# A hybrid decoder block on one core: a new order for the opening, and one output row stored in halves

## The chip, the cores and the metric

The kernel runs on one core of a Trainium2 chip. The metric is the device time of one execution in microseconds; the median of three runs of the kernel before is 907.87 us (907.3 to 908.28). The profile is of one further execution. Engines are named as the profile names them: PE is the matrix engine (TensorE), PEld its weight loads, DVE is VectorE, ACT is ScalarE, POOL is GpSimd, SP issues most transfers.

## The reference, cut to what matters

One residual block over 1024 tokens of width 1024, all in float32. The opening computes the modulation of the conditioning vector and the normalised, modulated input h; everything else starts from one large projection of h.

```python
def rmsnorm(x, g):
    r = lax.rsqrt(jnp.mean(xf * xf, axis=-1, keepdims=True) + NORM_EPS)
    return (xf * r).astype(x.dtype) * g

mod = c @ w_ada[l] + b_ada[l]
shift, scale, gate = jnp.split(mod, 3, axis=-1)
h = rmsnorm(x, norm_g[l]) * (1.0 + scale[:, None, :]) + shift[:, None, :]
proj = h @ w_in[l]
q, k, v, g_attn, xr, g_rnn, m_attn, m_rnn = jnp.split(proj, SPLIT_POINTS, axis=-1)
q = partial_rope(q, positions)           # ang = positions * inv_freq; cos, sin
k = partial_rope(k, positions)
# sliding-window attention with sinks, a conv and an RG-LRU, gates,
# two projections, one output projection
x = x + gate[:, None, :] * (merged @ w_out[l])
return rmsnorm(x, final_g)
```

## The kernel before, in words

**Numbers.** A float32 product is made of three products of rounded operands: each operand is split into a high part (hh for h, wh for weights) and a rest (hl, wl), and PE computes hh x wh, hh x wl and hl x wh. A product is of 128 x 128 weights with 512 columns. ACT (or POOL) makes the high part with a cast, DVE the rest with a subtraction. Weights come by half chunks of 128 x 512 in tiles named r.

**The opening** (lines 186 to 550) has its order written out by hand for all five engines: each engine executes its instructions in the order in which the code calls them, and waits where an operand is not there. Nothing overtakes.

- SP loads eight tiles of x (128 tokens each), a table of small parameters (pk_t), then in turns weight halves and the modulation matrix (wada, two tiles of 512 KB for each of eight blocks kc of 128 features). The positions (posr_t) come over POOL's queue.
- For each tile i of x: ACT squares and sums it (`square`, L365), DVE forms the mean plus epsilon (`mean`, L368), ACT takes the root (`root`, L372), DVE the reciprocal and scales the tile (`scaled`, L376 and L378), or, for the tiles in DIAG, scales an identity matrix (L382). PE transposes the tile in eight pieces into two sets of four PSUM banks (`flip`, L395, L397), and after two tiles ACT or DVE evicts the four banks (`out_of`, L403, L405) into xT.
- The conditioning vector is broadcast by PE (L264) and copied by DVE into c_bc. For each kc, DVE multiplies two wada tiles with it and sums (`modulate`, L275): one gives the shift, one the scale. The shift of kc 0 is made by PE instead (L451), in bank bk0. ACT turns them into a shift and a gain for each feature (`scales_of`, L280, L282).
- `hi_parts(kc)`: ACT writes the high part of h (L411, L413; in two halves of 512 tokens for kc below 4) and then h itself in place (L415). `lo_parts(kc)`: DVE writes the rest (L472, L475).
- `first(kc, terms, cs)`: PE multiplies feature block kc with the weights of four starting column chunks c = 0 to 3. Chunks 2 and 3 collect in the banks bk, chunks 0 and 1 in the banks pmain, which also serve the transposes. The first weight halves of the chunks serve kc 0 to 3, the second halves kc 4 to 7; the second ones are cast by ACT: chunk 0 ahead of kc 4's h, chunks 1 to 3 behind kc 5's h.
- KEEP_BUSY products with zeros (L454) stand on PE between the transposes and the first product.

**The angles.** POOL reduces the rope angles to one turn in 36 small operations (L305 to L356). The generator `angles()` is advanced by `turn(n)`: three at a time among the tiles, and the rest behind POOL's casts of two weight halves. ACT then takes the sine (L526), on its queue between h of kc 4 and the scales of kc 5. POOL stores the result and loads the tables that the rope needs.

**The end.** The eight output rows of 128 tokens are finished one after another; row 6 and row 7 overlap. ACT scales the right half of row 6 (L1965), DVE its left half (L1969), SP stores the row in one transfer. Row 7 is then scaled and stored in halves.

Of the kernel before, what the change touches and what calls it, by code (L numbers as in the profile page):

```python
# [22 lines left out]
P = 128  # L23
S = 1024
D = 1024
# [22 lines left out]
DIAG = 0, 2, 4  # L48
KEEP_BUSY = 4
# [5 lines left out]
def tile_hybrid_block(ctx, tc, x, pk, rows, posr, posi, c_row, w_ss, w_gate, w_main, w_v,  # L55
# [135 lines left out]
    with ExitStack() as st:  # L191
# [6 lines left out]
        dma(posr_t[:], posr, G)  # L198
# [34 lines left out]
        load_ss(0)  # L233
        for c in (0, 1):
            load_s(c, 0)
# [13 lines left out]
        warm = sp.tile([P, 1], F32, name="warm")  # L249
        V.memset(one_row[:], 1.0)  # L250
        zero = rbig[:, :HALF]
# [27 lines left out]
        def scales_of(kc):  # L279
            A.activation(shf[:, kc:kc + 1], mods[:, kc:kc + 1] if kc else bk[0][:, 0:1],  # L280
                         AF.Identity, bias=pcol(PK_BSH, kc))
            A.activation(gsc[:, kc:kc + 1], mods[:, 8 + kc:9 + kc], AF.Identity,  # L282
                         scale=pcol(PK_NG, kc), bias=bng[:, kc:kc + 1])

# [82 lines left out]
        def mean(i):  # L367
            V.tensor_scalar(out=rr[:, i:i + 1], in0=ss[:, i:i + 1], scalar1=1.0 / D, scalar2=EPS,  # L368
                            op0=ALU.mult, op1=ALU.add)

        def root(i):
            A.activation(rr[:, i:i + 1], rr[:, i:i + 1], AF.Sqrt)  # L372
# [16 lines left out]
        def flip(i):  # L389
            for kc in range(KC):  # L390
# [16 lines left out]
        def hi_parts(kc, between=lambda: None):  # L407
# [6 lines left out]
            between()  # L414
# [10 lines left out]
        late = {1: [lambda: V.tensor_copy(c_bc[:, SL[0]], psc[0]),  # L425
                    lambda: V.tensor_copy(c_bc[:, SL[1]], psc[1])],
                3: [lambda: out_of(0, 0, V), lambda: out_of(0, 1, V)],
                4: [lambda: out_of(0, 2, V), lambda: out_of(0, 3, A)],
                5: [lambda: out_of(1, 0, V), lambda: out_of(1, 1, V)],
                6: [lambda: out_of(1, 2, A), lambda: out_of(1, 3, A),  # L430
                    lambda: V.scalar_tensor_tensor(
                    out=bng[:], in0=pk_t[:, PK_BSC:PK_BSC + 8], scalar=1.0,
                    in1=pk_t[:, PK_NG:PK_NG + 8], op0=ALU.add, op1=ALU.mult)]}
# [12 lines left out]
        scaled(7)  # L446
        for p in range(4):
            out_of(2, p, A)
        flip(7)
        for k in range(KC):  # L450
            T.matmul(bk[0][:, 0:1], wada[0, 0][:, k * P:(k + 1) * P], pcol(PK_C, k),  # L451
                     start=(k == 0), stop=(k == KC - 1))
        for i in range(KEEP_BUSY):
            T.matmul(bk[1], zero[:, 0:P], zero, start=True, stop=True)  # L454
        for c in (2, 3):
            cast_s(c, 0, G)
        cast_s(0, 0)
        turn()
        modulate(0, (1,))
        for p in range(2):  # L460
            out_of(3, p, A)
        scales_of(0)
        hi_parts(0, lambda: cast_s(1, 0))
        for c in (2, 3, 0):
            rest_s(c, 0)
        modulate(1)
        csn = sp.tile([P, 3, 64], F32, name="csn")

        def lo_parts(kc):
            if kc < 4:  # L470
                for hf in range(2):
                    V.tensor_tensor(out=hl[kc][hf], in0=xT[kc][:, SL[hf]],  # L472
                                    in1=f32(hh[kc][hf]), op=ALU.subtract)
# [1583 lines left out]
```

## Time and profile before

| | |
|---|---|
| median of three runs | 907.87 us |
| the profiled execution | 907.33 us, its span 905.5 us |
| PE busy | 894.3 us, 99% |
| first product of the projection | 23.44 us |
| PE without a gap from | 28.07 us to the end of the opening |
| sine of the angles on ACT | 41.99 us |
| last product | 898.23 us |

Times in rows are microseconds from the span's start: start, duration, engine, line, operation, output and input by the program's names. A bracket tells how long the engine had been idle before, and what released it. In a table by stretches, each engine's busy time is followed by its number of instructions in brackets; the last three numbers are the granted PE clock, the share of the transfer engines and GB/s.

### The profile page before, as it was taken

The numbers are of one execution on the slowest core, as the hardware profiler recorded it, in microseconds if no ns is written. First come the engines' busy times: TensorE is split into PE (matmuls) and PEld (weight loads), VectorE is DVE, ScalarE is ACT, GpSimd is POOL, SyncE is SP. The second block draws the span as 40 slices with busy tenths as digits, with TensorE's granted clock in tenths as the row PEclk, the third lists the DMA queues.
The fourth block names the chain that finished last, engine by engine and source line by source line (L and its number), as shares of the span: only waits on it lengthen the run. The fifth ranks groups of instructions, "written<-read, shape, count | busy, mean of one in ns | idle before, by whom it ended". The sixth has DMA issues, their size and how long they took to land.

```text
span 905.5 us, 12663 instructions
## 1 busy us (share of the span) xinstructions
PE 894.3 (99%) x4259; PEld 746.1 (82%) x4259; DVE 718.6 (79%) x1073; ACT 567.2 (63%) x1098; POOL 121.1 (13%) x216
## 2 busy tenths in 40 slices
PE   8999999999999999999999999999999999999996
PEld 6789888888888888888888888888888888888885
DVE  6987688978669875987788597999999847569755
ACT  7965554654566855786585884888888732115435
POOL 6520241200000000000000002343433300000000
PEclk9999999999999999999999999999999999999999
DMA  9828489772435354354446367996656289316504
GB/s 356 338 69 285 165 256 321 256 234 95 151 128 182 121 208 135 124 183 163 158 140 214 105 203 248 349 404 208 215 199 207 74 310 363 140 47 234 207 1 186
DMA packets 87205, 180.74 MB, mean 200 GB/s; under 512 B 8626, under 2 KB 29122, under 8 KB 87140
## 3 DMA queue, kind: packets, MB, share of 16 engines
q1 hardware_dynamic: 83056, 167.07, 52.3%
q0 software_dynamic: 3936, 12.59, 4.3%
q8 instruction: 34, 0.56, 0.3%
q14 instruction: 31, 0.25, 0.1%
q10 hardware_dynamic: 148, 0.27, 0.1%
HBM read 121.34 MB, written 58.95 MB: 199 GB/s over the span
## 4 chain that ended last, share of the span: by engine, by line
PE 93%; DVE 4%; ACT 2%; issue 1%; DVEq 0%; ACTq 0%
PE bk L709 48%; PE rp L173 13%; PE out L1861 6%; PE pmain L173 5%; PE pgate L1025 5%; PE s_ps L1330 3%; PE pv L1403 3%; PE pmain L485 2%; PE bk L485 2%; PE pt L1369 1%; PE pmain L1580 1%; PE pmain L1579 1%; PE pmain L1578 1%; ACT jk L1879 1%; DVE xo L1875 1%
## 5 line engine op out<-in xcount | busy, mean ns | idle before, releaser
L709 PE MATMUL bk<-nh,wh 128*128 128x512 f32 x368 | 143.3, 389 | 0.0
L709 PE MATMUL bk<-nl,wh 128*128 128x512 f32 x368 | 143.2, 389 | 0.0
L709 PE MATMUL bk<-nh,wl 128*128 128x512 f32 x368 | 98.4, 389 | 0.0
L111 DVE TENSOR_TENSOR wl<-r,wh 128x512 fp32r<-128x512 f32 x109 | 75.0, 695 | 24.0 <-ACT wh L105 23.7
L105 ACT CAST wh<-r 128x512 fp32r<-128x512 f32 x107 | 65.5, 618 | 31.0 <-PE rp L173 11.1
L709 PEld LDWEIGHTS bk<-nh,wl 128*128 128x128 f32 x368 | 69.1, 188 | 14.4
L709 PEld LDWEIGHTS bk<-nl,wh 128*128 128x128 f32 x368 | 69.1, 188 | 14.2
L709 PEld LDWEIGHTS bk<-nh,wh 128*128 128x128 f32 x368 | 69.1, 188 | 14.2
L709 PE MATMUL bk<-hl,wh 128*128 128x512 f32 x184 | 71.6, 389 | 0.0
L709 PE MATMUL bk<-hh,wh 128*128 128x512 f32 x184 | 71.6, 389 | 0.0
L111 DVE TENSOR_TENSOR wl<-ws,wh 128x512 fp32r<-128x512 f32 x76 | 52.1, 687 | 7.1 <-ACT wh L105 7.0
L62 POOL DMA_DIRECT2D yh_d<-av x1 | 0.6, 567 | 371.3 <-ACT av L1092 371.3
L1355 ACT ACTIVATE p<-p,small 128x129 f32<-128x129 f32 x128 | 50.0, 396 | 0.0
L709 PE MATMUL bk<-hh,wl 128*128 128x512 f32 x184 | 49.2, 389 | 0.0
L105 ACT CAST wh<-ws 128x512 fp32r<-128x512 f32 x76 | 46.0, 614 | 4.3 <-PE bk L709 2.1
L709 PEld LDWEIGHTS bk<-hh,wl 128*128 128x128 f32 x184 | 34.5, 188 | 7.2
L709 PEld LDWEIGHTS bk<-hl,wh 128*128 128x128 f32 x184 | 34.6, 188 | 7.1
L709 PEld LDWEIGHTS bk<-hh,wh 128*128 128x128 f32 x184 | 34.5, 188 | 7.1
L1330 PEld LDWEIGHTS s_ps<-ks,qs 128*128 128x128 f32 x256 | 34.4, 189 | 3.7 <-DVE p L1345 1.1
L1330 PE MATMUL s_ps<-ks,qs 128*128 128x256 f32 (+1 forms) x256 | 35.3, 280 | 0.6 <-DVE p L1345 0.6
L709 PE MATMUL bk<-hha,wh 128*128 128x512 f32 x92 | 35.8, 389 | 0.0
L709 PE MATMUL bk<-hla,wh 128*128 128x512 f32 x92 | 35.8, 389 | 0.0
(378 smaller groups left out, 2289.3 us busy)
## 6 DMA issues: line engine op xcount, KB each, us to landing
r<-w_main SPq DMA_DIRECT2D x100, 256.0 KB, 4.2
wada<-w_ss SPq DMA_DIRECT2D x16, 512.0 KB, 9.0
qs<-q_d SPq DMA_DIRECT2D x16, 512.0 KB, 4.9
wo_d<-wr SPq DMA_DIRECT2D x28, 256.0 KB, 3.0
wo<-wo_d SPq DMA_DIRECT2D x14, 512.0 KB, 5.1
ks<-k_d SPq DMA_DIRECT2D x12, 384.0 KB, 4.3
xt<-x SPq DMA_DIRECT2D x8, 512.0 KB, 7.0
sma_d<-c SPq DMA_DIRECT2D x16, 256.0 KB, 4.4
```

What stands on the lines that cost most here:

```text
L105: A.copy(dst[0][:], src)
L111: V.tensor_tensor(out=dst[1][:], in0=src, in1=f32(dst[0][:]), op=ALU.subtract)
L173: mm = T.matmul(ps[hf], ww, xx[kc][hf], start=(kc == 0 and ww is w_h and xx is xh), stop=(kc == KC - 1 and xx is xl))
L485: T.matmul(starts[c][hf], ww[:, c0:c0 + P], xh[kc][hf], start=(kc == 0 and t_ == "h"), stop=(kc == KC - 1 and t_ == "l"))
L709: W["pe"] = T.matmul(ps, ww[:, kc * P:(kc + 1) * P], b[kc][i], start=(first and n == 0), stop=(n == 11), skip_group_check=not first)
L1025: W["pe"] = T.matmul(ps[:, SL[hf]], ww[:, c0:c0 + P], xx_[:, SL[hf]], start=(ic == 0 and i == 0), stop=(ic == 1 and i == 2))
L1330: W["pe"] = T.matmul(o, qs[:, j, qc], ks[:, kb:n % 2 + 2, b, :], start=(b == 0), stop=(b == 1))
L1355: A.activation(px[:, j, :], px[:, j, :], AF.Exp, bias=sm[:, 0, j:j + 1], accum_out=sm[:, 1, j:j + 1])
L1369: W["pe"] = T.transpose(pt[:, j, :], px[:, j, 0:P], ident[:])
L1403: W["pe"] = T.matmul(pv[:], b, m[:].rearrange("p j q -> p (j q)"), start=(i == 0), stop=(i == len(prods) - 1))
L1578: T.matmul(o, hh[kc][th][:, ts_], wh[:, cols], start=(kc == 0), stop=False)
L1861: T.matmul(o, a[k][x_][:, p * P:(p + 1) * P], b[k][y_][:, cols], start=(first and k == 0 and i == 0), stop=(k == 3 and i == 2), skip_group ...
```

## The change

- `mean` is gone: `root` computes the square root of sum / D + eps itself, with eps in a small tile, and follows its square directly on ACT.
- The order among the tiles of x: roots in groups, evictions in other places, two diagonal tiles in place of three, two filler products in place of four. `flip` writes a bank's two halves in sequence.
- The shift of kc 0 is computed by PE ahead of tiles 6 and 7, in a bank of pmain, and finished by ACT behind the evictions.
- The first h (kc 0) is made, and multiplied, by halves of 512 tokens; POOL casts the first weight halves of all four chunks, and computes bng.
- The positions are loaded over SP's queue; all angles stand behind POOL's four casts.
- Row 6 is stored in two halves, the right one first.

The places at which instructions move, engine by engine. POOL, from its setup to the first angles (posf, ang, t, a, sa, sb, sc are the angles' tiles; wh are high parts of weights). Before:

```order
L62 DMA posr_t<-posr 128x65
masks.py:197 MEMSET ident 128x128
masks.py:199 ISA
masks.py:199 AFFINE_SELECT ident<-ident 128x128
L305 CAST posf<-posr_t 128x64
L307 TENSOR_SCALAR ang<-posf,posr_t 128x64
L291 TENSOR_SCALAR t_324<-ang 128x64
```

and further on, in the middle of the angles:

```order
L297 TENSOR_TENSOR a_411<-a_356,t_409 128x64
L322 TENSOR_SCALAR tmp<-t_409 128x64
L224 CAST wh<-r 128x512 x2
L326 TENSOR_TENSOR sa<-sa,tmp 128x64
L322 TENSOR_SCALAR tmp<-t_409 128x64
```

With the change:

```order
masks.py:199 AFFINE_SELECT ident<-ident 128x128
L469 TENSOR_SCALAR bng<-pk_t 128x8
L471 TENSOR_TENSOR bng<-bng,pk_t 128x8
L223 CAST wh<-r 128x512 x4
L313 CAST posf<-posr_t 128x64
L315 TENSOR_SCALAR ang<-posf,posr_t 128x64
L299 TENSOR_SCALAR t_463<-ang 128x64
L305 TENSOR_TENSOR a_465<-ang,t_463 128x64
```

The load is gone from this queue, and the 18 operations that stood ahead of the two casts stand behind four.

ACT, from the last root to kc 1's scales (hha and hhb are the high parts of h by token halves). Before:

```order
L372 ACTIVATE rr<-rr 128x1 x2
L403 COPY xT<-bk_68 128x2x256
L403 COPY xT<-bk_69 128x2x256
L403 COPY xT<-bk_70 128x2x256
L403 COPY xT_194<-bk_71 128x2x256
L105 CAST wh<-r 128x512
L403 COPY xT<-pmain 128x2x256 x2
L280 ACTIVATE shf<-bk_68,pk_t 128x1
L282 ACTIVATE gsc<-mods,bng,pk_t 128x1
L411 ACTIVATE hha_161<-xT,shf,gsc 128x512
L411 ACTIVATE hhb_162<-xT,shf,gsc 128x512
```

With the change:

```order
L376 ACTIVATE rr<-ss,eps 128x1
L407 COPY xT_194<-pmain 128x2x256
L407 COPY xT<-pmain 128x2x256
L407 COPY xT<-bk_70 128x2x256
L407 COPY xT<-bk_68 128x2x256
L407 COPY xT_194<-bk_71 128x2x256
L407 COPY xT<-bk_69 128x2x256
L282 ACTIVATE shf<-pmain,pk_t 128x1
L286 ACTIVATE gsc<-mods,bng,pk_t 128x1
L481 ACTIVATE hha_161<-xT,shf,gsc 128x512
L407 COPY xT<-pmain 128x2x256
```

Six evictions now stand between the last root and the first shift, the last two tiles' evictions and the second half of h behind it.

PE, from the shift's products to the first products with h. Before:

```order
L395 MATMUL pmain<-ident,xt 128x128 x16
L451 MATMUL bk_68<-pk_t,wada 128x1 x8
L454 LDWEIGHTS rbig
L454 MATMUL bk_69<-rbig 128x512
```

With the change, and with the buffers' numbers (pmain_198 holds the shift and half of each transposed tile):

```order
L461 MATMUL pmain_198<-pk_t_75,wada_232 128x1 x8
L399 MATMUL pmain_197<-ident_76,xt_223 128x128 x4
L399 MATMUL pmain_198<-ident_76,xt_223 128x128 x4
L399 MATMUL pmain_197<-ident_76,xt_225 128x128 x4
L399 MATMUL pmain_198<-ident_76,xt_225 128x128 x4
L468 LDWEIGHTS rbig_78
L468 MATMUL bk1_69<-rbig_78 128x512
```

The shift's products have moved ahead of tiles 6 and 7, whose pieces share a bank with it. PE's order from the second product with kc 1's rest on, ACT's and DVE's from kc 2's scales on, are as they were, but for a few casts and additions near the end of the kernel that the scheduler has placed otherwise.

The diff, cut to its core:

```diff
-DIAG = 0, 2, 4
-KEEP_BUSY = 4
+DIAG = 0, 2
+KEEP_BUSY = 2
...
-        dma(posr_t[:], posr, G)
...
         load_ss(0)
+        dma(posr_t[:], posr)
         for c in (0, 1):
             load_s(c, 0)
...
+        V.memset(eps[:], EPS)
...
-        def mean(i):
-            V.tensor_scalar(out=rr[:, i:i + 1], in0=ss[:, i:i + 1], scalar1=1.0 / D, scalar2=EPS,
-                            op0=ALU.mult, op1=ALU.add)
-
         def root(i):
-            A.activation(rr[:, i:i + 1], rr[:, i:i + 1], AF.Sqrt)
+            A.activation(rr[:, i:i + 1], ss[:, i:i + 1], AF.Sqrt, scale=1.0 / D, bias=eps[:])
...
-            for kc in range(KC):
+            for kc in (0, 4, 1, 5, 2, 6, 3, 7):
...
-        turn(3)
...
-        for i in range(8):
-            square(i)
-            mean(i)
-            if i:
-                root(i - 1)
-                scaled(i - 1)
-                if i < 6:
-                    turn(3)
-                flip(i - 1)
-            for f in late.get(i, ()):
-                f()
-        root(7)
+        norm(0, 1)
+        scaled(0)
+        scaled(1)
...
+        norm(7)
+        evict(1, v=(0, 1), a=(3, 2))
         scaled(7)
-        for p in range(4):
-            out_of(2, p, A)
+        m00 = starts[1][1][:, 0:1]
+        for k in range(KC):
+            T.matmul(m00, wada[0, 0][:, k * P:(k + 1) * P], pcol(PK_C, k),
+                     start=(k == 0), stop=(k == KC - 1))
+        evict(2, a=(2, 0, 3, 1))
+        shift_of(0, m00)
+        flip(6)
         flip(7)
...
-        for c in (2, 3):
+        for c in (2, 3, 0, 1):
             cast_s(c, 0, G)
-        cast_s(0, 0)
         turn()
         modulate(0, (1,))
...
+        hi_half(0, 0)
+        first(0, "hw", (2, 3), (0,))
+        evict(3, a=(0,), v=(2,))
+        affine_half(0, 0)
+        modulate(1, (0,))
+        rest_s(0, 0)
+        rest_s(1, 0)
+        modulate(1, (1,))
+        first(0, "hw", (0, 1), (0,))
+        hi_half(0, 1)
...
     A.activation(xo[6][:, RIGHT], xo[6][:, RIGHT], AF.Copy, scale=r6)
+    dma(out[6 * P:7 * P, RIGHT], xo[6][:, RIGHT])
...
-    dma(out[6 * P:7 * P, :], xo[6][:])
+    dma(out[6 * P:7 * P, LEFT], xo[6][:, LEFT])
```

More of the change, by code (lines that the diff above doesn't have):

```diff
@@ L449, in tile_hybrid_block @@
+        for k in range(KC):
[4 more added lines that the diff above has]
+        flip(6)
         flip(7)
-        for k in range(KC):
-            T.matmul(bk[0][:, 0:1], wada[0, 0][:, k * P:(k + 1) * P], pcol(PK_C, k),
-                     start=(k == 0), stop=(k == KC - 1))
         for i in range(KEEP_BUSY):
             T.matmul(bk[1], zero[:, 0:P], zero, start=True, stop=True)
-        for c in (2, 3):
+        G.tensor_scalar(out=bng[:], in0=pk_t[:, PK_BSC:PK_BSC + 8], scalar1=1.0, scalar2=None,
+                        op0=ALU.add)
@@ L476, in lo_parts, with first @@
                                 op=ALU.subtract)
-        def first(kc, terms, cs=range(N_ST)):
+        def first(kc, terms, cs=range(N_ST), halves=range(2)):
             for c in cs:
@@ L483, in first @@
                     ww, xh = {"h": (h, hh), "w": (l, hh), "l": (h, hl)}[t_]
[L484 removed]
+                    for hf in halves:
                         T.matmul(starts[c][hf], ww[:, c0:c0 + P], xh[kc][hf],
```

94 lines of the change are left out of this document (57 added, 37 removed).

## The prediction

> **What bounds the kernel now.** I read the page's busy shares first, then TensorE's (PE) timeline of the opening, then the engines that end its waits.
>
> ```profile
> span 905.5 us, 12663 instructions
> PE 894.3 (99%) x4259; PEld 746.1 (82%) x4259; DVE 718.6 (79%) x1073; ACT 567.2 (63%) x1098; POOL 121.1 (13%) x216
> PE 93%; DVE 4%; ACT 2%; issue 1%; DVEq 0%; ACTq 0%
> ```
>
> PE is busy 99% of the span and holds 93% of the chain that ended last. So an edit counts only if it moves PE's first matmuls, opens a gap in PE, or moves what follows PE at the end. PE's matmul order behind the first three contraction chunks (kc 0 to 2) does not change.
>
> ```profile
> 23.44 0.47 PE L485 MATMUL bk<-hha,wh 128*128 128x512 f32 x1 [0.68 <-ACT hha L411]
> ...
> 28.07 0.39 PE L485 MATMUL bk<-hha,wh 128*128 128x512 f32 x1
> 28.30 0.40 PE L485 MATMUL bk<-hhb,wh 128*128 128x512 f32 x1
> ...
> 48.04 0.62 PE L485 MATMUL pmain<-hh,wh 128*128 128x512 f32 x2
> ```
>
> The input projection starts at 23.44. The row at 28.07 is its 15th matmul; from there on one starts every 0.227 us (28.07 to 28.30, and 88 steps from 28.07 to 48.04). With no gap at all the stream would have begun at 28.07 - 14 x 0.227 = 24.9: I call that the effective start. The row at 48.04 is matmul 102 (counted from 0): the first of kc 4 for column chunk 1, and the first that needs that chunk's second weight half.
>
> **The opening itself.** Its chain is squares and roots on ScalarE (ACT), scaling on VectorE (DVE), transposes on PE, evictions, first h.
>
> ```profile
> 7.98 1.06 ACT L365 ACTIVATE junk<-xt 128x1024 bf16<-128x1024 f32 x1 [0.93 <-DMA xt<-x]
> 8.95 0.18 ACT L365 ACTIVATION_READ_ACCUMULATOR junk<-xt 128x1 f32 x1
> ...
> 17.29 0.20 ACT L372 ACTIVATE rr<-rr 128x1 f32<-128x1 f32 x1 [0.47 <-DVE rr L368]
> 17.86 2.06 ACT L403 COPY xT<-bk 128x512 f32<-128x512 f32 x4 [0.36 <-PE bk L395]
> ...
> 884.84 0.29 ACT L1890 ACTIVATE rbig<-rbig 128x1 f32<-128x1 f32 x1
> ```
>
> The mean goes into the root, and each root stands right behind its square. The last row is such a root at the kernel's end: 0.29 us. A square with its accumulator read takes 1.15 (7.98 to 9.13), so a tile takes about 1.42. Six tiles from 7.98 and one eviction (2.06 / 4 = 0.51) end at 17.0, against 17.49 (17.29 + 0.20). Six evictions follow (3.1), then the first shift (0.2): 20.3.
>
> ```profile
> 18.23 1.97 PE L395 MATMUL pmain<-ident,xt 128*128 128x128 f32 x16
> 21.74 1.02 PE L454 MATMUL bk<-rbig 128*128 128x512 bf16 x4
> ```
>
> The shift's eight small products now stand ahead of the last two tiles' transposes, in a bank these need, so half of tile 6's transposes wait for the shift: 20.3. Left are one and a half tiles (1.97 / 2 each, 1.5) and two filler matmuls (half of 1.02): 22.3 for the first matmul, 1.1 earlier. Its h half is ready at about 21.5 and waits.
>
> ```profile
> 14.44 1.28 DVE L405 COPY xT<-pmain 128x512 f32<-128x512 f32 x2
> ...
> 18.27 0.75 DVE L378 TENSOR_SCALAR xt<-xt,rr 128x1024 f32<-128x1024 f32 x1
> 18.94 1.26 DVE L275 SCALAR_TENSOR_TENSOR jk<-wada,c_bc 128x1024 bf16<-128x1024 f32 x1
> 20.13 2.16 DVE L111 TENSOR_TENSOR wl<-r,wh 128x512 fp32r<-128x512 f32 x3
> ```
>
> DVE decides next. It scales tile 7 until about 18.8 (19.02 before), does the first modulation (1.26) and two low weight halves (0.7 each) to 21.4, evicts a bank when tile 7 is transposed (21.8 to 22.5, 0.64 as in the first row), then one modulation and two low halves: 25.1. Matmul 7 needs the last: effective start 25.1 - 7 x 0.227 = 23.5. **The opening alone is worth 1.4 us**, if nothing stalls later. Bounds: 2.6 (24.9 - 22.3, DVE not limiting) and 0 (DVE held 0.6 by each of the two casts that go to GpSimd, POOL). The rest costs nothing on PE: the transposes' new order, fewer diagonal multiplications (DIAG) and the sum bng on POOL lie ahead of the 22.3 beside ACT's chain.
>
> ```profile
> 4.70 0.94 SPq L62 DMA_DIRECT2D pk_t<-pk  x1
> 11.75 0.33 SPq L62 DMA_DIRECT2D r<-w_main  x1
> ...
> r<-w_main SPq DMA_DIRECT2D x1, 256.0 KB, 7.3
> ```
>
> The positions' load moves from POOL's queue into SP's, ahead of the first halves of chunks 0 and 1. A like load (first row) issues in 0.94. Chunk 0's half, issued at 11.75, lands at 19.05; up to 0.94 later is still ahead of the 20.1 at which DVE ends its modulation. Covered; without that cover it is the 0.94.
>
> **Where it is lost: the angles.** Of the 36 POOL operations that make the rope angles, 18 stood ahead of two weight casts and 18 behind; now all stand behind four casts.
>
> ```profile
> 6.32 0.46 POOL L307 TENSOR_SCALAR ang<-posf,posr_t 128x64 f32<-128x64 f32 x1
> ...
> 14.20 0.40 POOL L322 TENSOR_SCALAR tmp<-t 128x64 f32<-128x64 f32 x1
> 15.17 1.28 POOL L224 CAST wh<-r 128x512 fp32r<-128x512 f32 x2 [0.57 <-DMA r<-w_main]
> ...
> 20.45 0.78 POOL L291 TENSOR_SCALAR ra<-sa 128x64 f32<-128x64 f32 x1
> ...
> 31.97 1.03 POOL L356 TENSOR_SCALAR trn<-trn 128x128 f32<-128x128 f32 x1
> ```
>
> ```profile
> 5.90:14.70 8.80, 8.33 (x56) 6.36 (x56) 7.06 (x21) 7.75 (x20) 7.41 (x18) 1.00 1.02 401
> 20.40:33.00 12.60, 11.42 (x54) 8.37 (x54) 12.21 (x19) 11.95 (x22) 11.56 (x13) 1.00 1.03 402
> 109.90:120.40 10.50, 10.50 (x48) 8.71 (x47) 10.40 (x18) 7.65 (x14) 9.12 (x17) 1.00 0.69 230
> ```
>
> The windows' counts (third bracket DVE, fifth POOL) are the argument. From 5.9 to 14.7, while DVE copies from PSUM, scales and idles, POOL does 18 operations in 8.63 us: 0.48 each. From 20.4 to 33.0 DVE runs operations with two SBUF inputs (19, five of them accumulator reads), and POOL does 13 in 12.6 us: 0.97 each, one per DVE operation. From 109.9 to 120.4 it is 17 beside 18, on tiny 128x8 operands: lockstep again, so size is not the cause. In the changed kernel all 36 fall into this second regime.
>
> ```profile
> 41.99 0.31 ACT L526 ACTIVATE csn<-trn 128x128 f32<-128x128 f32 x1
> ...
> 45.52 1.65 ACT L105 CAST wh<-r 128x512 fp32r<-128x512 f32 x3
> ```
>
> ```profile
> 44.03 1.22 DVE L275 SCALAR_TENSOR_TENSOR jk<-wada,c_bc 128x1024 bf16<-128x1024 f32 x1
> ...
> 46.16 1.90 DVE L111 TENSOR_TENSOR wl<-r,wh 128x512 fp32r<-128x512 f32 x3 [0.90 <-ACT wh L105]
> ```
>
> The fourth cast (0.61 each, behind DVE's modulation) ends near 21.4. DVE then has 24 two-input operations and one eviction up to its modulation of kc 6, which ended at 45.2 and ends at about 46.5 now (0.5 for its later kc 2, 0.8 for POOL beside 11 more: the three at 20.13 took 2.16 with POOL, the three at 46.16 took 1.90 without). After that DVE needs casts that ACT does behind the sine, so it idles and POOL runs at 0.48. POOL: 26 done by 46.5, 10 x 0.48 more: **51.5**. The sine has waited until then; it ran at 41.99 with its input ready at 33.0 (31.97 + 1.03). Queued behind it on ACT are kc 5's scales, its h, and the three casts. So chunk 1's cast moves with it: 4.14 behind the sine (45.52 + 0.61 - 41.99), now 55.6. PE wanted it at 48.04, 1.9 after its end at 46.13. **Delay of PE against before: 51.5 - 41.99 - 1.9 = 7.6**; the opening's 1.4 only makes PE stand 9.0 instead. Bounds: 0.48 throughout gives 38.7, no stall; 0.97 to the end gives 56.3.
>
> ```profile
> 62.95 0.68 DVE L617 TENSOR_TENSOR c<-pmain,ctab 128x512 f32<-128x512 f32 x1
> ```
>
> Behind the angles in POOL's queue stand the transfers of the rope tables. They move by the sine's 9.5, and their first use, the row above, which waited for nothing, moves with PE by 9.3: no second stall.
>
> **The clock.** A gap of 9 us has its own price.
>
> ```profile
> 1.38 4.55 PE L256 MATMUL bk<-rbig 128*128 128x512 bf16 x12 [1.38 <-DVE warm L258]
> ...
> 898.23 0.28 PE L1861 MATMUL out<-wo,ml 128*128 128x256 f32 x1
> ```
>
> ```profile
> 903.00:904.00 1.00, 0.00 (x0) 0.00 (x0) 0.00 (x0) 0.00 (x0) 0.00 (x0) 0.50 0.75 273
> 900.00:901.00 1.00, 0.00 (x0) 0.00 (x0) 0.94 (x3) 0.72 (x1) 0.00 (x0) 1.00 0.00 0
> 901.00:902.00 1.00, 0.00 (x0) 0.00 (x0) 0.00 (x0) 0.00 (x0) 0.00 (x0) 1.00 0.98 393
> ```
>
> PE's last matmul is that of 898.23; the granted clock (third number from the end) is 1.00 to 902 and 0.50 from 903. At the start, 12 products of 512 columns take 4.55, a pitch of 0.38 where 0.227 is full speed: about 8 of them at twice the pitch, some 1.7 us lost until the clock is up. PE idle for 9 us falls to half and pays that again: **1.7**, bounds 0 and 2.0.
>
> **The end.** Row 6 is stored in two halves. Its right half is ready early, in a stretch where the DMA engines are idle (DMA share 0.00 from 900 to 901).
>
> ```profile
> 898.70 0.72 ACT L1965 ACTIVATE xo<-xo,rbig 128x512 f32<-128x512 f32 x1 [0.23 <-DVE rbig L1964]
> ```
>
> It can go at 899.4. Then 256 KB fewer stand before row 7's, 0.67 us at 393 GB/s; but row 7's own halves go no earlier, as their scaling is not touched. Bounds 0 and 0.67; I take **0.3**, halfway.
>
> **Sum.** On the profiled execution (907.33 us, span 905.5): +7.6 +1.7 -0.3 = +9.0, 916.3. The median of the runs shown is 907.87, 0.54 higher, inside their spread.
>
> The Trainium skill, "SBUF — State Buffer", section "SBUF: two separate sides", says that VectorE and GpSimd share a port pair as an exclusive lock: an operation with two SBUF inputs, or a GpSimd operation, holds it for its whole length and the other blocks fully. The trace agrees for POOL (13 beside 14). For DVE it does not: three operations take 0.26 longer beside POOL, 0.09 each, not POOL's 0.48.
>
> **Rivals.**
> - Faster: the angles are ready in time, because POOL slips more than one operation between two of DVE. The sine must not start later than 41.99 + 1.9 - 1.4 = 42.5, which leaves 21.1 us for 36, 0.59 each. Then 907.33 - 1.4 - 0.3 = 905.6. For it: the 0.48 of the early window, and a POOL that is busy 13% of the span. Against: both lockstep windows, at 0.97 and 0.62 with the smallest operands. Chance 0.09.
> - Slower by less: 0.70 per operation, midway. Sine at 46.6, PE 4.6 - 1.9 = 2.7 late after a gap of 4.1, at the edge of the clock's fall (half of 1.7): 910.6. Chance 0.10.
> - Slower by more: POOL stays at 0.97 after DVE has gone idle. Sine at 56.3, 14.3 - 1.9 + 1.7 - 0.3: 921. Against: the early window. Chance 0.06.
> - DVE waits out each POOL operation: 24 x (0.48 - 0.09) = 9.4 later, 925.7. That is the skill's lock to the letter, and the rows above are against it. Chance 0.02.
> - No change: something ahead of the sine that I price at nothing is itself late, or the angles miss by the 1.7 that the opening gains. Chance 0.03.
> - The forecast: 0.70.
>
> **Numbers.** Faster or slower counts from 0.2%, 1.8 us, which a measurement can tell from no change. Faster 0.09, same 0.03, slower 0.88. The forecast's own range is 913.5 to 918.5: sine 1.5 either way, the clock's 0 to 2.0. To hold 8 in 10 the range takes in the second rival and stops short of the third: 909.5 to 920.
>
> **What would show it.** POOL's angles begin near 21.4 and end near 51.5, at 0.9 to 1.0 each until 46; ACT idles about 9 us ahead of the sine, released by POOL; DVE idles ahead of its low halves; PE has one gap of about 9 us ahead of kc 4's second chunk, near 46.7 to 55.7, with a granted clock below 1 in it and behind; the first matmul is near 22.3. A sine near 41 and no gap would refute the whole; a gap without a fall of the clock, only the 1.7.

## The result, and the profile after

The changed kernel takes 917.33 us (median of five runs, 916.64 to 918.17); the kernel before takes 907.9 in the same set (907.3 to 908.93). The ratio is 1.0104, with a 95% interval from 1.0089 to 1.0119: 1% slower. The forecast was 916.3, in a range of 909.5 to 920. The profiled execution took 917.33 too, with a span of 915.5 against 905.5.

The page of the changed kernel, with its span, busy times and the chain that ended last:

```profile
span 915.5 us, 12637 instructions
PE 896.7 (98%) x4248; PEld 748.0 (82%) x4249; DVE 718.5 (78%) x1066; ACT 568.2 (62%) x1096; POOL 131.5 (14%) x219
PE 89%; POOL 3%; DVE 3%; DMA 2%; ACT 2%; issue 1%; SPq 0%; DVEq 0%; ACTq 0%
```

PE is busy for about as long as before. What is new is 3% of POOL in the chain, which runs through the angles, until now on no path that counted, from 20.8 to 51.3. PE's timeline in the changed kernel shows where PE stood because of it:

```profile
46.59 0.62 PE L509 MATMUL pmain<-hh,wh 128*128 128x512 f32 x2
...
47.50 0.61 PE L509 MATMUL pmain<-hl,wh 128*128 128x512 f32 x2
55.51 1.22 PE L509 MATMUL pmain<-hh,wh 128*128 128x512 f32 x2 [7.39 <-ACT wh L105]
56.52 1.05 PE L509 MATMUL pmain<-hh,wl 128*128 128x512 f32 x2
...
61.96 0.63 PE L509 MATMUL pmain<-hh,wh 128*128 128x512 f32 x2
```

Followed backwards: the row at 55.51 waits 7.39 us for a cast of ACT, the cast stands on ACT behind the sine, and the sine waits for POOL. The rows of ACT, DVE and POOL in the changed kernel:

```profile
51.34 0.31 ACT L556 ACTIVATE csn<-trn 128x128 f32<-128x128 f32 x1 [8.13 <-POOL trn L364]
...
54.85 1.64 ACT L105 CAST wh<-r 128x512 fp32r<-128x512 f32 x3
```

```profile
55.48 1.90 DVE L111 TENSOR_TENSOR wl<-r,wh 128x512 fp32r<-128x512 f32 x3 [8.30 <-ACT wh L105]
```

```profile
20.81 0.69 POOL L313 CAST posf<-posr_t 128x64 f32<-128x64 int32 x1
...
46.16 1.26 POOL L347 TENSOR_SCALAR tmp<-a 128x64 f32<-128x64 f32 x1
47.50 0.32 POOL L350 TENSOR_TENSOR sc__461<-sc__461,tmp 128x64 f32<-128x64 f32 x1
...
50.77 0.53 POOL L364 TENSOR_SCALAR trn<-trn 128x128 f32<-128x128 f32 x1
```

POOL's first angle starts at 20.81, behind two casts that wait for a weight half to land (18.97), and its last ends at 51.30. Up to 47.42 it did 29 of the 36 (0.92 each); from 47.50, with DVE idle since 47.18, the last seven took 0.54 each. From 23.44 on, when DVE is past its wait for the transposes, it is 24 operations of POOL beside 24 of DVE with two inputs in SBUF. A TENSOR_TENSOR of 128x64 takes 0.32 alone and 0.5 to 1.2 beside DVE.

For the account, PE's rows of the kernel before that answer to these, and a landmark at which the projection's first stage is over:

```profile
46.68 0.62 PE L485 MATMUL pmain<-hh,wh 128*128 128x512 f32 x2
...
52.12 0.62 PE L485 MATMUL pmain<-hh,wh 128*128 128x512 f32 x2
...
68.44 0.28 PE L1578 MATMUL pmain<-wh,hha 128*128 128x256 f32 x1
```

| landmark on PE | before | after | later by |
|---|---|---|---|
| first product of kc 4 (chunk 0) | 46.68 | 46.59 | -0.09 |
| first product with chunk 1's second half | 48.04 | 55.51 | 7.47 |
| first product of kc 5 | 52.12 | 61.96 | 9.84 |
| first product of the next stage (pmain<-wh,hha) | 68.44 | 78.29 | 9.85 |
| last product | 898.23 | 908.82 | 10.59 |
| end of the span | 905.5 | 915.5 | 10.0 |

So the opening, with all its new order, is worth 0.09; the wait for the angles costs 7.56; the 18 products behind it, at the lower clock, cost 2.37; 0.74 is lost between the end of the first stage and the last product; and the end is 0.59 shorter. Each profile is one execution: the sixth experiment below has the opening of the kernel before, unchanged, and its profile reaches kc 4 at 46.11, 0.57 earlier. So a few tenths in the opening cannot be told from one pair of profiles; 7.56 and 2.37 can.

### The profile page after: what moved, and what is told of

The parts are those of the page before. It is cut to its first block, busy times and chain, and to the rows that moved or that the text cites. A ratio compares the mean times of both kernels' runs of the same rounds, so it can differ in the third digit from the quotient of the medians.

```text
span 915.5 us, 12637 instructions
## 1 busy us (share of the span) xinstructions
PE 896.7 (98%) x4248; PEld 748.0 (82%) x4249; DVE 718.5 (78%) x1066; ACT 568.2 (62%) x1096; POOL 131.5 (14%) x219
## 4 chain that ended last, share of the span: by engine, by line
PE 89%; POOL 3%; DVE 3%; DMA 2%; ACT 2%; issue 1%; SPq 0%; DVEq 0%; ACTq 0%
PE bk L739 48%; PE rp L173 13%; PE out L1891 6%; PE pmain L173 5%; PE pgate L1055 5%; PE s_ps L1360 3%; PE pv L1433 3%; PE pt L1399 1%; PE bk L509 1%; PE pmain L509 1%; DMA xt<-x 1%; PE pmain L1610 1%; PE pmain L1609 1%; PE pmain L1608 1%; DMA r<-w_main 1%
```

## The experiments

Each is compared with runs of the kernel before on the same chip: medians 907.32 (experiments 1, 2, 4 and 5), 907.47 (3, 6, 7 and 8), 907.72 (9 and 10) and 907.69 (11 and 12).

**1. The angles back to an early place.** The changed kernel, with the positions loaded over POOL's queue at the start and 18 angle operations ahead of bng and the four casts.

```diff
         posr_t = sp.tile([P, 65], I32, name="posr_t")
+        dma(posr_t[:], posr, G)
...
         load_ss(0)
-        dma(posr_t[:], posr)
...
+        turn(18)
         G.tensor_scalar(out=bng[:], in0=pk_t[:, PK_BSC:PK_BSC + 8], scalar1=1.0, scalar2=None,
```

> The changed kernel with one part undone: the positions are loaded over POOL's queue at the start again, and 18 of the 36 angle operations stand ahead of POOL's sums and casts. Theory (the angles behind the casts run in lockstep with DVE and hold the sine): the angles end near 38, the sine does not wait, PE has no gap ahead of kc 4's second chunk. The opening's effective start was 24.83 with the change and 24.9 before, so it gives 0.1, the row in halves 0 to 0.3: 907.0, between 906 and 908. Rival (the order by token halves or the clock's fall in the opening is what costs): the angles matter little and it stays above 914.

Measured: 908.99 (908.5 to 910.49), ratio 1.0018 (1.0009 to 1.0027). It is 1.67 above the kernel before of its own set, where the changed kernel was 9.4 above: 7.8 of the 9.4 us are gone. The last angle and the sine in this kernel:

```profile
35.47 0.53 POOL L364 TENSOR_SCALAR trn<-trn 128x128 f32<-128x128 f32 x1
```

```profile
43.02 0.31 ACT L557 ACTIVATE csn<-trn 128x128 f32<-128x128 f32 x1
```

The sine waits for nothing, and PE has no gap at kc 4. The lateness of the angles is the cause, and the rival (some other wait of the new order) falls. But the expected 907.0 was missed by 2: the rest of the change does not bring the 1.4 that the forecast gave the opening. It costs 1.7. That is taken up below.

**2. Only the angles late.** The kernel before, with all 36 angles behind its two casts, and nothing else of the change.

```diff
-        turn(3)
...
-                if i < 6:
-                    turn(3)
```

> The kernel before with one part of the change alone: all 36 angle operations behind POOL's two casts (the positions still come over POOL's queue). Theory: POOL starts them at 16.5 and does one for each DVE operation with two SBUF inputs, 29 up to 45.9, the last 7 alone at 0.45: sine at 49.2, PE 7.2 - 1.9 = 5.3 late, a gap of 5.3 in PE, and the clock's fall for 2.4 more: 915, between 911 and 917. Rival (POOL's operations cost only their own 0.48): angles done at 33.8, nothing changes, 907.9.

Measured: 914.9 (913.93 to 915.52), ratio 1.0077 (1.006 to 1.0094): as expected, to 0.1. The sine and PE in this kernel:

```profile
48.80 0.31 ACT L523 ACTIVATE csn<-trn 128x128 f32<-128x128 f32 x1 [6.86 <-POOL trn L356]
```

```profile
52.97 1.22 PE L482 MATMUL pmain<-hh,wh 128*128 128x512 f32 x2 [4.25 <-ACT wh L105]
```

The place of the angles makes 7.6 of loss by itself, from a program that has none of the rest. From both sides, alone and undone, the cause is the same.

**3. Only the sine moved.** The changed kernel, with the sine behind ACT's casts of chunks 1 to 3; the angles stay as late as they are.

```diff
-        A.activation(csn[:, 0:2, :].rearrange("p a t -> p (a t)"), trf, AF.Sin)
-        A.activation(csn[:, 2, :], csn[:, 1, :], AF.Copy, scale=-1.0)
...
         for c in range(1, N_ST):
             cast_s(c, 1)
             rest_s(c, 1)
+        A.activation(csn[:, 0:2, :].rearrange("p a t -> p (a t)"), trf, AF.Sin)
+        A.activation(csn[:, 2, :], csn[:, 1, :], AF.Copy, scale=-1.0)
...
```

> The changed kernel with one edit: the sine, its copy and the two DMAs of its result stand behind ScalarE's three casts of chunks 1 to 3 instead of ahead of them; the angles stay where the change put them, so they still end at about 51.3. The theory (what TensorE waits for is not the angles but ScalarE's casts, queued behind the sine): the cast of chunk 1 no longer waits, TensorE restarts within about 2 us of 48, the clock does not fall for long, the sine comes at about 55 and the tables of rope about 4 us later than in the changed kernel; 910 (907.5 to 913). The rival (the late angles pass on to rope by the tables and cost the same there): 915 or more, with a new wait at the first operation of rope.

Measured: 912.72 (912.48 to 916.5), ratio 1.0069 (1.0053 to 1.0086). The gap at kc 4 is gone, at the upper end of the expected range, and another wait stands in its place. PE's and DVE's rows in this kernel:

```profile
59.94 0.61 PE L509 MATMUL pmain<-hh,wl 128*128 128x512 f32 x2
62.91 1.22 PE L509 MATMUL pmain<-hl,wh 128*128 128x512 f32 x2 [2.35 <-DVE hl L499]
```

```profile
55.35 1.23 DVE L499 TENSOR_TENSOR hl<-xT,hh 128x1024 fp32r<-128x1024 f32 x1 [1.58 <-ACT xT L418]
```

The sine (at 51.69, still waiting for POOL) holds up the h of kc 6 and 7, DVE gets them late, and PE waits for the last low part. So the step "queued behind it on ACT are the casts" is right: with other work behind the sine, 4.2 of the 9.4 go (5.25 above the kernel before is left). The rest, but for the 1.7 of the first experiment, follows the sine to whatever stands behind it.

**4. The clock held up through the gap.** The changed kernel, with 34 products of zeros, accumulated, between chunk 0 and chunk 1 of kc 4.

```diff
-        chunks(4)
+        chunks(4, cs=(0,))
+        for i in range(34):
+            T.matmul(starts[0][i % 2], zero[:, 0:P], zero, start=False, stop=False,
+                     skip_group_check=True)
+        chunks(4, cs=(1, 2, 3))
```

> The changed kernel, and 34 products of zeros (512 columns, about 0.22 us each, 7.3 us) that PE adds to an accumulating bank between kc 4's first and second chunk, where it otherwise stands idle for 7.4 us. Nothing of the work changes. Theory (the 2.4 us that PE loses behind the gap are the clock's): granted clock 1.00 throughout, 917.3 - 2.4 = 914.9. Rival (PE is slow behind the gap for its operands, or the fillers are too long): 917.3 or more.

Measured: 918.41 (917.42 to 918.82), ratio 1.0116 (1.0101 to 1.0131). The expected gain of 2.4 did not come. The windows of the changed kernel and of this one show that the clock did what was meant (the granted clock is the third number from the end):

```profile
52.00:54.00 2.00, 0.00 (x0) 0.00 (x0) 0.00 (x0) 1.93 (x4) 1.82 (x3) 0.87 0.10 31
54.00:60.00 6.00, 4.49 (x11) 3.48 (x12) 4.48 (x7) 5.75 (x9) 0.61 (x1) 0.50 0.33 115
60.00:62.00 2.00, 2.00 (x10) 1.62 (x9) 2.00 (x4) 1.00 (x2) 0.86 (x1) 0.93 0.00 0
```

```profile
46.00:60.00 14.00, 12.97 (x57) 7.34 (x57) 4.81 (x7) 7.98 (x13) 7.56 (x14) 1.00 0.16 54
```

And PE's rows with a wait in this kernel show where the gain went:

```profile
56.02 0.73 PE L509 MATMUL pmain<-hh,wh 128*128 128x512 f32 x2 [0.96 <-ACT wh L105]
...
65.96 0.62 PE L509 MATMUL pmain<-hh,wh 128*128 128x512 f32 x2
...
68.95 0.73 PE L509 MATMUL pmain<-hl,wh 128*128 128x512 f32 x2 [0.56 <-DVE hl L499]
...
107.49 0.50 PE L743 MATMUL bk<-nh,wh 128*128 128x512 f32 x1 [0.50 <-ACT bk L795]
```

The product at 65.96 is that at 67.41 in the changed kernel: PE is 1.45 ahead there, though its sine came 0.5 later (51.86). Then it stands for DVE's last low part. In the changed kernel DVE ends that part at 68.38 (67.16 + 1.22), and PE wants it at 69.67, 1.29 later. So of the 2.37 that the slow clock costs there, 1.08 is time for which PE would have stood anyway. The lead melts further: 0.26 at the start of the next stage (78.03 against 78.29), and behind the wait at 107.49 PE is 0.48 later than in the changed kernel (107.01). The first wait is for DVE, which runs late behind the sine. The second is for an eviction of ACT, which had itself stood 4.08 for a weight half (95.29) and 2.89 for a store of v (105.84); whether that comes of the sine is not shown. From 575 to 849 the two kernels are level within 0.1, and the 1.2 by which this one ends later is lost at 849 to 853, in the output products, where PE waits 0.62 for ACT. That the fall of the clock has no price at all is not shown, since the sine itself came 0.5 later in this kernel; what is shown is that PE's 2.37 could not be had back as 2.37. One thing more: PE is busy through the gap here, and POOL, with DVE idle, still does nine angles from 47.17 to 51.82, 0.52 each. So it is not PE's rest that makes POOL faster there.

**5. Narrow angles.** The changed kernel, with the angle operations on 8 columns in place of 64 or 128; the other angles are left out. The edit, cut to one of its lines:

```diff
-            G.tensor_tensor(out=t[:], in0=a, in1=b, op=op)
+            G.tensor_tensor(out=t[:, :8], in0=a[:, :8], in1=b[:, :8], op=op)
```

> The changed kernel with the angle operations on 8 of their 64 or 128 columns: the rest of the angles is left out (taken as zero). The number of POOL operations is the same. Theory (lockstep: one operation for each of DVE, whatever its size): 26 done by 47.1 as before, then 10 alone at about 0.3 instead of 0.45: sine near 49.7, 915.6. Rival (POOL is slowed in proportion to its own work): the operations shrink with their size, the sine is ready near 40 and the time is near 907.

Measured: 912.75 (912.54 to 913.33), ratio 1.0056 (1.0041 to 1.0071), between the two theories. The sine and some of POOL's rows in this kernel:

```profile
47.16 0.31 ACT L557 ACTIVATE csn<-trn 128x128 f32<-128x128 f32 x1 [4.71 <-POOL trn L365]
```

```profile
27.30 0.23 POOL L331 TENSOR_SCALAR tmp<-t 128x8 f32<-128x8 f32 x1
27.62 0.48 POOL L335 TENSOR_TENSOR sb<-sb,tmp 128x8 f32<-128x8 f32 x1
28.18 1.09 POOL L331 TENSOR_SCALAR tmp<-t 128x8 f32<-128x8 f32 x1
...
43.47 1.06 POOL L353 TENSOR_TENSOR trn<-ft,sc__462 128x8 f32<-128x8 f32 x1
...
46.88 0.24 POOL L365 TENSOR_SCALAR trn<-trn 128x8 f32<-128x8 f32 x1
```

An operation that takes some 0.24 alone still takes 1.0 to 1.3 in 13 of 26 places beside DVE; in the others it takes 0.2 to 0.7, and now and then two fit between two operations of DVE: 26 in the 22.7 us from 23.21 to 45.84, 0.87 each. With the full width, DVE's wait for the transposes left out, it is 24 in the 24.0 us from 23.44 to 47.42, 1.00 each. So the pace is mostly DVE's, not POOL's, but it is not strictly one for one.

**6. The last row in halves, alone.** The kernel before with the last edit only.

```diff
+    dma(out[6 * P:7 * P, RIGHT], xo[6][:, RIGHT])
...
-    dma(out[6 * P:7 * P, :], xo[6][:])
+    dma(out[6 * P:7 * P, LEFT], xo[6][:, LEFT])
```

> The kernel before with one edit: row 6 is stored in two halves. The forecast's term: 0.3 below the kernel before, so about 907.0 (906.6 to 907.3). The rival, that the last transfer is not set by the bytes of row 6: the same as before, 907.3.

Measured: 906.81 (906.19 to 908.13), ratio 0.9993 (0.9984 to 1.0002): 0.66 below, with an interval that just reaches no change. The traces say it more sharply: from the last product to the end of the span it is 7.27 before (898.23 to 905.5), 6.76 here (897.64 to 904.4) and 6.68 in the changed kernel. The edit is worth 0.5 to 0.6.

**7 and 8. Filling the opening.** What the opening lost, in PE's and ACT's rows of the changed kernel:

```profile
17.38 1.95 PE L461 MATMUL pmain<-pk_t,wada 128*128 128x1 f32 x16 [1.30 <-ACT xT L407]
19.19 3.54 PE L399 MATMUL pmain<-ident,xt 128*128 128x128 f32 x16
...
22.88 0.58 PE L509 MATMUL bk<-hha,wh 128*128 128x512 f32 x1
...
25.35 0.50 PE L509 MATMUL pmain<-hha,wl 128*128 128x512 f32 x1 [0.97 <-DVE wl L111]
```

```profile
25.89 1.23 ACT L407 COPY xT<-pmain 128x512 f32<-128x512 f32 x2 [1.97 <-PE pmain L509]
```

Sixteen transposes took 3.54 where the same sixteen took 1.97 before. The windows say why:

```profile
18.00:20.00 2.00, 2.00 (x17) 2.00 (x18) 2.00 (x4) 1.88 (x6) 1.03 (x2) 0.83 1.05 425
20.00:22.00 2.00, 2.00 (x11) 2.00 (x10) 1.40 (x2) 0.83 (x2) 1.89 (x3) 0.50 1.03 414
```

The granted clock fell to a half in the middle of the opening. Both attempts stand on top of the first experiment. The seventh experiment adds four products of zeros ahead of the shift's one-column products; the eighth also emits kc 0's second half of h and its evictions ahead of the first products.

```diff
+        for i in range(4):
+            T.matmul(starts[0][0], zero[:, 0:P], zero, start=True, stop=True)
```

```diff
         affine_half(0, 0)
+        hi_half(0, 1)
+        evict(3, a=(1, 3))
+        affine_half(0, 1)
...
         first(0, "hw", (0, 1), (0,))
-        hi_half(0, 1)
         first(0, "hw", (2, 3), (1,))
-        evict(3, a=(1, 3))
-        affine_half(0, 1)
```

> The first experiment (the changed kernel with the angles early, 909.0) with four 512-column products of zeros into a bank that is written afresh later, ahead of the products of the shift, where TensorE idles 1.3 us. Theory (the granted clock falls at about 19.3 because TensorE idles and then runs one-column products): the clock stays at 1.00, the sixteen flips of 3.03 take 1.97, the first product of the main stage starts about 1 us earlier; 908.0 (907.5 to 908.5). Rival (the fall has another cause than TensorE's idleness, or VectorE's wl is what comes last at 25.0): 909.0, no change.

> The experiment with the four filling products, and with the evictions p1 and p3 of the second half, its h and its affine step emitted ahead of the first products, so that ScalarE's evictions no longer wait for products into the same tiles. Theory (the second loss of the opening is that order): ScalarE's wait of 1.97 at 25.89 goes, h of the second half comes up to 1.4 us earlier, TensorE's 0.4 wait for it is gone; 907.3 (906.3 to 908.0). Rival (TensorE's own work sets the end of the opening by then): 0.0 to 0.2 below the experiment before.

Measured: 909.8 (908.94 to 910.96), ratio 1.0028 (1.0017 to 1.0038); and 909.05 (907.27 to 911.85), ratio 1.002 (1.001 to 1.0029). Both missed. In the seventh the clock fell all the same. Its products wait for an eviction of the very bank that they write, so that they fill little of the idle time:

```profile
17.21 1.02 PE L461 MATMUL pmain<-rbig 128*128 128x512 bf16 x3 [1.12 <-DVE xT L409]
...
19.78 3.61 PE L399 MATMUL pmain<-ident,xt 128*128 128x128 f32 x16
```

In the eighth, where they wait just so (1.02), the clock stayed up, the sixteen transposes took 2.02 and kc 4 began at 45.86: 0.8 ahead of the kernel before, 0.25 ahead of the sixth experiment's profile. Why the clock fell in the one and not in the other is taken up in the last section. But the lead was gone at 60, where PE waits 0.5 for DVE's last low part, and at 69.15, where PE stands 0.7 later than before.

**9 and 10. Two edits to get the lead through.** On top of the last one: DVE makes the last low part ahead of the operands nl; then also the eviction that the change had given to DVE goes back to ACT.

```diff
+    lo_parts(7)
     make_operands(0)
     chunks(5)
-    lo_parts(7)
```

```diff
-        evict(3, a=(0,), v=(2,))
+        evict(3, a=(0, 2))
```

> The eighth experiment (angles early, filling products, new order of emission; 909.05) with one edit: VectorE makes the low part of the last group of w_main rows ahead of the two operands nl (2.36 in the trace) instead of behind them. Theory (of the 1.6 that this program stands behind the kernel before, 0.8 is TensorE's wait for that low part at 60, since VectorE runs 1 us later than in the kernel before): TensorE's wait at 60 goes, 908.2 (907.7 to 908.6). Rival (VectorE's lateness only passes on to rope's operations, which TensorE waits for at 69): 909.0.

> The experiment before with one more edit: the one eviction that the change gave to VectorE in the opening (0.69, and 0.73 of waiting for TensorE's transposes ahead of it) goes to ScalarE with the other three. Theory (VectorE and ScalarE hand the lateness to and fro by the products with the modulation weights, and it began with that eviction): VectorE's last modulation and its last low part come up to 1.2 earlier, the wait at rope goes as well; 907.6 (907.0 to 908.2). Rival (ScalarE gets as late by the eviction as VectorE gains): the same as the experiment before.

Measured: 908.97 (907.88 to 911.09), ratio 1.0017 (1.0008 to 1.0027); and 908.08 (906.68 to 909.9), ratio 1.0003 (0.9995 to 1.0012). The ninth went as its rival said: the wait at 60 (0.55 in the eighth) goes, and that at rope grows from 0.17 to 0.92.

```profile
69.10 0.36 PE L1611 MATMUL pmain<-wh,hha 128*128 128x256 f32 x1 [0.92 <-DVE c L650]
```

With the eviction off DVE as well, no wait of 0.2 or more is left on PE from 26 to 500: kc 4 begins at 45.83 and the next stage at 67.67, 0.8 ahead of the kernel before (0.2 to 0.3 ahead of the sixth experiment's profile). So DVE's lateness did begin with that eviction (0.69, and 0.73 of waiting in front of it); in between, DVE and ACT hand it on, since ACT's scales wait for DVE's modulation sums and DVE's low parts for ACT's h. Yet the median is that of the kernel before. The profiled execution, 906.68, was the shortest of its eleven, so the trace shows the best case; and even there the lead is gone by the last product (898.21 against 898.23). Nearly all of it, 0.7, goes at one place, and it is the place at which the changed kernel loses its 0.74: PE's wait for DVE in the attention at 565.03 (575.61 in the changed kernel), which the kernel before does not have. It begins 18 us earlier, where DVE waits for a transfer (th<-sgr_d). The rows are those of the kernel before, of the changed kernel and of the tenth experiment:

```profile
546.38 1.23 DVE L1089 TENSOR_TENSOR rz<-rz,th 128x1024 f32<-128x1024 f32 x1 [0.33 <-DMA th<-sgr_d]
```

```profile
557.25 1.23 DVE L1119 TENSOR_TENSOR rz<-rz,th 128x1024 f32<-128x1024 f32 x1 [1.36 <-DMA th<-sgr_d]
...
575.61 1.22 PE L1360 MATMUL s_ps<-ks,qs 128*128 128x256 f32 x8 [0.47 <-DVE p L1375]
```

```profile
546.71 1.23 DVE L1122 TENSOR_TENSOR rz<-rz,th 128x1024 f32<-128x1024 f32 x1 [1.36 <-DMA th<-sgr_d]
...
565.03 1.22 PE L1363 MATMUL s_ps<-ks,qs 128*128 128x256 f32 x8 [0.44 <-DVE p L1378]
```

In the tenth SP issues this transfer 0.7 earlier than in the kernel before, with PE's lead, and it lands 0.3 later. What DVE makes of it is stored over POOL's queue, and by the profile DVE waits for that store to land (5.0) four operations ahead of the one that PE waits for. The wait for th is 0.3 to 0.8 in the four profiles on the kernel before and 0.8 to 1.9 in the ten on the changed one, although the order of the instructions there is the same; why the transfer lands later is not settled.

**11 and 12. The mean and the halves alone; the clock or the waits.** First the kernel before with the mean in the root and row 6 in halves; then the tenth experiment without the filling products.

```diff
-            A.activation(rr[:, i:i + 1], rr[:, i:i + 1], AF.Sqrt)
+            A.activation(rr[:, i:i + 1], ss[:, i:i + 1], AF.Sqrt, scale=1.0 / D, bias=eps[:])
```

```diff
-        for i in range(4):
-            T.matmul(starts[0][0], zero[:, 0:P], zero, start=True, stop=True)
```

> The kernel before with the two parts of the change that move no other work: the mean goes into the root (VectorE's eight operations go), and row 6 is stored in halves. Theory (in the opening of the kernel before TensorE waits 0.9 in all for VectorE's scaled rows, and each of the eight is some 0.1 to 0.2 of VectorE): 906.5 (906.0 to 907.0), the first product up to 0.5 earlier. Rival (the opening is held by ScalarE and the arrival of the weights, and nothing but the halves counts): 906.8, as with the halves alone.

> The tenth experiment without the four filling products, which waited for an eviction themselves and so filled little. Theory (the fall of the clock at 19 to 23 comes of TensorE's idle time ahead of the one-column products; some 0.5 of products behind that wait tip it): the clock falls again, the flips take 3.0 to 3.5 and the time is 908.7 (908.2 to 909.5). Rival (the filling products are worth nothing, order alone keeps the clock): 908.1 or up to 0.4 less, flips 2.0.

Measured: 907.12 (906.55 to 907.67), ratio 0.9994 (0.9985 to 1.0002); and 907.98 (906.99 to 911.03), ratio 1.0004 (0.9995 to 1.0012). The mean brings nothing that shows over the halves (0.57 below the kernel before, against 0.66), and the first product starts at 23.47, where it started at 23.44 (22.88 in the sixth experiment's profile): in all three ACT's h is what comes last there, not DVE. In the twelfth the clock fell again in the profiled execution, and it cost nothing that shows:

```profile
20.00:22.00 2.00, 2.00 (x15) 1.90 (x14) 2.00 (x5) 1.82 (x4) 1.91 (x3) 0.72 1.04 422
22.00:24.00 2.00, 2.00 (x7) 1.39 (x5) 2.00 (x4) 1.73 (x4) 1.75 (x4) 0.50 1.02 398
```

```profile
24.92 0.47 PE L510 MATMUL pmain<-hha,wh 128*128 128x512 f32 x1 [0.28 <-ACT xT L407]
```

PE waits 0.28 for ACT's eviction here; in the tenth experiment, at full clock, it waited 1.34 for the same eviction (24.85). kc 4 begins at 45.89 against 45.83. PE's slow transposes only filled a wait. The clock was up in all three profiles that had the filling products in this order, and that was worth nothing.

No version beats the kernel before by more than its runs tell apart; the two lowest are those with row 6 in halves on top of the opening of the kernel before.

## Why the prediction was right, point by point

- **The angles** (delay of PE against before 7.6): right, 7.47 (48.04 to 55.51). Forecast and measured: first angle near 21.4 and 20.81, the sine at 51.5 and 51.34, chunk 1's cast ended at 55.6 and 55.46, PE's gap 46.7 to 55.7 and 47.96 to 55.51. The two regimes are as forecast, 0.97 and 0.48 against 0.92 and 0.54. "26 done by 46.5" was 29 done by 47.42: DVE stood idle for 1.44 around 22, and POOL ran four operations at some 0.4 in that stretch. That the sine came out within 0.2 is in part luck: three operations more were done than forecast, but 0.9 later, and the last ones took 0.54 where 0.48 was forecast. So is the start of the first angle: what held POOL's last two casts was a weight half that landed at 18.9 (a wait of 2.41), not DVE's modulation. The step that mattered, that ACT's casts stand behind the sine, is shown by moving the sine. DVE's last modulation ahead of the gap ended at 47.18, 1.9 later than before, of which 1.44 is its wait for PE. The rule of the Trainium skill, "SBUF — State Buffer", section "SBUF: two separate sides", that the lock blocks either side in full would by the forecast's estimate have made DVE 9.4 later; beside the angles the trace agrees with it for POOL alone.
- **The opening alone** (1.4): wrong, 0.09 in the changed kernel, 0.85 at the best in the tenth experiment, and nothing of it at the end. The 1.4 would have put kc 4 at 45.3; the five profiles with the opening as the change has it (the changed kernel and, but for the place or width of the angles or the sine's, experiments 1, 3, 4 and 5) have it at 46.0 to 47.3; the unchanged opening has 46.68 and 46.11. What failed is the step that carried 22.3 for the first matmul into 25.1 for DVE's last low half. PE ended its transposes 1.6 late since the clock fell, which the forecast did not look for in the opening; DVE's eviction waited for them 1.44. DVE's first two low halves took 2.10 (19.30 to 21.40) where 1.4 was forecast, beside POOL's casts, and ended at the forecast 21.4 only because DVE had started on them 0.7 early. ACT's evictions of the second half were emitted behind products into the same banks, a wait of 1.97 that the forecast did not count, and h of kc 1 came late by it. And the lead did not simply stay: DVE ran so close to its limit that 1 us of its lateness came back as a wait of PE at 60 to 69. In the sum the miss cost nothing, since PE stands until 55.5 for the angles in either case, as the forecast said: it stood 7.55 instead of 9.0.
- **The clock** (1.7, bounds 0 to 2.0): mis-sized. By PE's rows it cost 2.37, since the pitch was doubled until about 60.3, 4.8 us behind the restart. What it costs the kernel is less, 1.3 by the slack of the last low part; filling the gap won nothing in the end. The step that failed is the one that took the price from the twelve products at the kernel's start. The price is no constant: the same 18 products cost 2.37 in the second experiment too and 1.69 in the fifth, and the twelve at the start take 4.22 to 5.30 from profile to profile (the last section says why). And the term left out that the other engines were late behind the sine as well.
- **Row 6 in halves** (0.3): right in sign; 0.5 to 0.6 in the traces, near the upper bound of 0.67.
- **Rope's tables**: right, no second stall (DVE's first use of them waits for nothing).
- **Sum** (+9.0): +10.0 by the spans, 9.4 by the medians. By the landmarks it is 7.5 for the angles, 2.4 for the clock, 0.7 and -0.6 for the end. The 0.7, lost in the attention at 575.61, was in no term: it comes of a transfer that lands late, as told at the tenth experiment. So the forecast is 1.0 short by the spans: 0.7 too little for the clock and 0.7 not foreseen, less the 0.3 that the end gave beyond its term.

The rivals: full or partial slipping of POOL (905.6, 910.6) needs 0.59 or 0.70 for each of the 36 operations, and it was 0.85 (0.73 even with 8 columns). A POOL that stays slow needs 0.97 with DVE idle, and it was 0.54. A DVE that waits out POOL needs 9.4 of lateness, and DVE was 1.9 late.

## What to carry to other kernels

Work that hangs on nothing is not free to move: ask what stands behind its consumer in that engine's queue, and how fast it runs in the company it will have there (the same operations took twice as long beside VectorE). Gains at the front of a tuned pipeline reach the end only if every engine that feeds it is as far ahead; look for the second engine, at its limit, that gives the lead back. Time that a slow clock costs is only lost where the engine would not have waited anyway.

## What the runs showed of the hardware that was not expected

- The granted clock fell at 19.34 us after only 1.3 us of PE idle time and 1.95 us of one-column products (16.1 to 19.3 together). It fell between 18 and 24 in all seven programs with the new opening but without filling products that helped (the changed kernel and experiments 1, 3, 4, 5, 7 and 12), in none of the three with filling products and the later order (8 to 10), and, at 22 to 27, in two of the four with the old opening (2 and 11; not in the kernel before and 6). The Trainium skill, "TensorE: Matmul & The Clock Gate", section "What's actually happening", says that the activity window is about 3.4 us and runs freely, so that the same kernel behaves differently from run to run. The traces agree: within each profile every change of the clock lies a multiple of 3.41 us behind the first (in the changed kernel 5.68, 19.34, 22.75, 53.47 and 60.30).
- What counts in such a stretch can be read from the 14 profiles together. Cut into stretches of 3.41 us from the first change, and with PE's time in products of more than one column added up for each, every stretch at full clock with 1.27 us or less is followed by half clock, and every one with 1.85 or more by full clock; five lie between, and went either way. If one-column products are counted as well, stretches of 2.1 to 3.1 fell where one of 1.47 did not. So one-column products count for little or nothing, and whether a program falls depends on where its thin stretch lies between two borders: the seventh experiment had 1.01 in its thinnest stretch of the opening, the eighth 1.90. No experiment varied this alone.
- Recovery took 4.8 us in the changed kernel (55.51 to 60.30) and in the second experiment, and 3.2 and 3.3 in the third and the fifth, where PE restarted just behind a border. That agrees with the 3.4 us of busy time that the same section gives for it, if they are counted from the next border.
- GpSimd's pace followed VectorE's work: 0.54 for each operation with VectorE idle, 1.00 between VectorE's two-input operations, 0.87 there with 8 columns.
